# Low parts of weight blocks by a negated copy and an accumulating transfer, in a two-layer recurrent trunk

## The chip, the cores and the metric

The kernel runs on one core of a Trainium2 chip. The metric is the device time of one execution in microseconds (us); the median of several runs is compared. A core has five engines that run their own instruction streams in order and wait for each other by semaphores: TensorE (PE, matmuls), VectorE (DVE), ScalarE (ACT), GpSimd (POOL) and SyncE (SP). Transfers between the chip's memory (HBM) and the core's memory (SBUF) are issued by one of these engines into a queue and carried by 16 DMA engines.

## What is computed

The reference is one inference step of two layers on 1024 prompt tokens and 8 x 4 sample tokens (1056 columns in all), width 1024, in float32. Cut to what matters here:

```python
# layer 0, a gated linear recurrence (RG-LRU), width 1536
u = rmsnorm(x, g0) @ a_w_in            # 1024 x 3072: branch and gate
xc = causal_conv(u[:, :1536])          # 4 taps
h = scan(a(xc), b(xc))                 # gates by 96 x 96 blocks
x = x + (h * silu(u[:, 1536:])) @ a_w_out      # 1536 x 1024
# layer 1, HGRN2: linear attention with decay, 8 heads of 128
q, f, v, gate = split(rmsnorm(x, g1) @ b_w_in) # 1024 x 4096
o = chunked_recurrence(silu(q), k(f), v, decay(f))
x = x + (norm(o) * silu(gate)) @ b_w_out       # 1024 x 1024
y = rmsnorm(x, gf)
```

## The kernel before

**Three products for one.** TensorE works on float32r operands, which keep fewer bits than float32. So each operand is split in two: the high part is the value rounded to float32r, the low part is the value minus the high part. A product is made of three matmuls into one bank (mm3, lines 253 to 257): high weights by high data (L255), high weights by low data (L256), low weights by high data (L257). The weights reach the core unsplit; the split is made on the chip, block by block.

**How a weight block becomes two.** A block is a tile of 128 partitions by up to 512 columns. A load brings it into a raw tile (wraw, a ring of NRAW = 3). ScalarE copies it into a float32r tile (whi, a ring of NW = 4): that is the high part. Then GpSimd subtracts the high part from the raw tile and writes the low part (wlo, a ring of NW = 4). Two places do this with GpSimd:

- `weights` (L382 to L403), for weights used in the ordinary way, in blocks of 512, 384 or 128 columns. Its argument e names the engine of the subtraction; without a word it is GpSimd (G). For the first two weight blocks of the program e is VectorE. Where `at` is given, the parts go to named homes instead of the rings; that is so for four weights at the start and two near the end.
- `split` within `seven` (L1446 to L1454), for layer 1's projections of heads 1 to 7. `seven` computes two 1024 x 128 projections (query and gate, or value and forget gate) with seven products of half size instead of eight, after Strassen and Winograd. Each product takes one raw block of 512 columns: some as loaded, some combined of others by VectorE (`combine`, L1456 to L1458), which writes over raw tiles. There are five raw slots, the ring of three and two halves of a row of R. GpSimd's subtraction is cut there into CUT = 2 halves of 256 columns.

Three more places split weights by GpSimd with code of their own (L561, L675, L1668).

**The order of the work.** Nothing is issued as it is written. Each operation is added to a `Flow` (L52) with its engine, an estimated duration, its emitter, the keys it reads and writes, and a priority. `Flow.run` plans the whole layer as a list schedule: it simulates the five engines and one serial transfer resource (250 KB per us, plus a latency of some 2.4 to 2.6 us), computes latest start times backwards from the end, uses them as priorities, repeats this, and at last tries 3000 random changes to the order of the first 60 us. Then the operations are issued in the planned order, engine by engine. The order on an engine is fixed from there; on the chip each instruction waits only for its semaphores. An operation that is late holds up what stands behind it on its engine. A change of the estimated costs or of the list of operations changes the planned order of everything.

**Who issues what.** Layer 0's loads and most stores are issued by SP (`dma`, L324), in SP's planned order; an issue that must wait for its tile to come free holds up the issues behind it. The loads of raw blocks in `seven` are issued by ScalarE (L1441), so there they stand in ScalarE's order. GpSimd issues no transfer.

**TensorE's part in layer 1.** Each of the seven products is 24 matmuls of 264 columns in two bank fills of 12. Three banks (NM7 = 3) take turns; VectorE's additions (`plus`, L1520, L1521) and ScalarE's copies (L1493) empty them. Between the products stand the bursts of small matmuls of the recurrence, at the places that the letters b in FQ, GV0 and GV (L30) mark: a query/gate pair and a value/forget pair alternate. The digits there are the order of the seven products; a block's split is issued NW = 4 products ahead of its use.

**The recurrence between.** Of each head, the rows are scaled level by level on VectorE (`scale`, L1057), turned with the help of transfers out of the core and back (`turned`, L1175), and ScalarE collects the turned keys (L1192). GpSimd raises small rows to a power for the norms (L463, L1317) and makes the masked values (L1216).

**The end.** The output projection of layer 1 adds its product, normalises and stores; there the late weights are split by L1668.

Of the kernel before, what the change touches and what calls it, by code (L numbers as in the profile page):

```python
# [18 lines left out]
AF = mybir.ActivationFunctionType  # L19
ALU = mybir.AluOpType  # L20
# [3 lines left out]
SEARCH = 3000  # L24
NW, NXO, NRAW = 4, 3, 3
K1 = 5
NMM = 3
HC = 2
NM7 = 3
FQ, GV0, GV = "12b675b43", "126b74b35", "126b754b3"  # L30
CUT = 2
SPOTS, SPOTS0, SPOTS1 = (-1, -1, 0, 2), (2, 5, -1, -1), (1, 5, 9, 13, 17, 20)
K2 = 8 - K1
RM, SM = 3, 6
# [189 lines left out]
def tile_trunk(ctx: ExitStack, tc: tile.TileContext, xT, prm, hc, w0, wg, wo0, w1, wo1, s_in,  # L224
               yT, h_out, c_out, sp_out, ss_out):
    nc = tc.nc
    V, S, G, T, Q = nc.vector, nc.scalar, nc.gpsimd, nc.tensor, nc.sync
# [83 lines left out]
    with ExitStack() as l0:  # L311
        pl = l0.enter_context(tc.tile_pool(name="l0", bufs=1, reuse_waits="tile"))
        fl = Flow("PE")
# [10 lines left out]
        def dma(dst, src, r=(), w=(), prio=5, kb=180, q=Q):  # L324
            fl.add("SP" if q is Q else "ACT", 0.45, lambda: q.dma_start(dst, src), r, w, prio, kb * (1.0 if r or fl.exact else 0.75))

        def act(n, emit, r, w, prio=5, more=0.0):
            fl.add("ACT", (0.09 + 0.00088 * n if fl.exact else 0.25 + 0.0007 * n) + more, emit, r, w, prio)

# [7 lines left out]
        def subtract(e, n, b, x, a, r, w, prio):  # L337

            emit = lambda: e.tensor_tensor(b, x, a.bitcast(F32), op=ALU.subtract)  # L339
            if e is G:  # L340
                pool(n, emit, r, w, prio)
            else:
                dve(n, emit, r, w, prio, True)
# [38 lines left out]
        def weights(src, n, prio=2, e=G, at=None, q=Q, own=()):  # L382

            own = iter(own)
            got = []
            for a in range(0, n, 512):
                m = min(512, n - a)
                raw, *rk = next(own, None) or next(raws)
                if at:
                    (hi, hk), (lo, lk) = ((o[:, a:a + m], k) for o, k in at)  # L390
                else:
                    (hi, hk), (lo, lk) = next(his), next(los)
                dma(raw[:, :m], src[:, a:a + m], (), rk, prio, m / 2, q)
                act(m, lambda hi=hi, raw=raw, m=m: S.copy(hi[:, :m], raw[:, :m]), rk, (hk,), prio)  # L394
                subtract(e, m, lo[:, :m], raw[:, :m], hi[:, :m], (*rk, hk), (lk,), prio)
                got.append((hi, lo, hk, lk))

            def get(k):
                q = slice((k % 4) * 128, (k % 4 + 1) * 128)
                hi, lo, hk, lk = got[k // 4]  # L400
                return hi[:, q], lo[:, q], (hk, lk)

            return get  # L403
# [457 lines left out]
        raw = (halves[1][:8], [slots[i] for i in (1, 4, 7, 2, 5, 8)] + [halves[1][8], free[8]], free[:8])  # L861
# [82 lines left out]
    with ExitStack() as l1:  # L944
        p1 = l1.enter_context(tc.tile_pool(name="l1", bufs=1, reuse_waits="tile"))
        last = {e: max(t[3] for t in fl.log if t[1] == e) for e in Flow.ENGINES}
        fl = Flow(side=0.4, busy={e: max(0.0, t - last["PE"]) for e, t in last.items()})
        banks8 = [next(mm) for _ in range(4)] + [next(hg) for _ in range(4)]
        mm, hg = cycle(banks8[:NMM]), cycle(banks8[NMM:])
        ts = cycle(ks)  # L950
# [3 lines left out]
        at = fixed("attn", [128, 8, 128], F32, p1)  # L954
# [466 lines left out]
        def seven(h, a, b, order, at=()):  # L1421
# [24 lines left out]
            def split(p):  # L1446
                (raw, rk), (hi, hk), (lo, lk) = slot[named[p]], next(his), next(los)
                act(512, lambda: S.copy(hi, raw), (rk,), (hk,), 2)  # L1448
                for i in range(CUT):
                    w = slice(i * (512 // CUT), (i + 1) * (512 // CUT))  # L1450
                    subtract(G, 512 // CUT, lo[:, w], raw[:, w], hi[:, w], (rk, hk), (lk,), 2)
                parts[p] = hi, lo, (hk, lk)
                if p not in (1, 2):
                    freed.append(slot[named[p]])  # L1454
# [15 lines left out]
            for c in order:  # L1470
# [8 lines left out]
                hi, lo, wk = parts[p]  # L1479
# [36 lines left out]
                n = steps.index(p) + NW  # L1516
# [72 lines left out]
        for k in range(H):  # L1589
            if k < 4:  # L1590
                olds = [("x", 1, k, x) for x in range(2)] + [("T", 1, i, k, x) for i in range(2) for x in range(2)]
            else:
                n, i = ((2, 0), (3, 0), (4, 0), (4, 1))[k - 4]
# [18 lines left out]
        def yparts(c):  # L1612
            return [(yh[k][:, chunk(c)], yl[k][:, chunk(c)], (("yh", k, c), ("yl", k, c))) for k in range(K1)]

# [21 lines left out]
        for n, (m, c) in enumerate([(m, c) for c in range(NCH) for m in range(2)] + [(m, c) for m in range(2, KD) for c in range(NCH)]):  # L1636
            if m not in ws2:
                at_ = None
                if m < 2:
                    at_ = [(flat[m + 2, 1][:, i * 640:i * 640 + 640], ("wt", m, i)) for i in range(2)]  # L1640
                    for _, k in at_:
                        inherit(k, [("T", m + 2, 1, j, x) for j in range(4) for x in range(2)])
                ws2[m] = weights(wo1[m][:, :128 * K1], 128 * K1, at=at_)
                for k in ykeys(Y2 + m, 0, TOK):
# [15 lines left out]
        for m in range(KD):  # L1660
            row = (xh, xl)[m // 4][4 + m % 4]
            hi, lo, hk, lk = row[:, :nl], row[:, nl:2 * nl], ("late", m, 0), ("late", m, 1)
            for k in (hk, lk):
                inherit(k, [("x", p, m % 4, x) for p in (2, 3) for x in range(2)])
            raw, rk = next(raws)
            dma(raw[:, :nl], wo1[m][:, 128 * K1:], (), (rk,), 1, nl / 2)
            act(nl, lambda hi=hi, raw=raw: S.copy(hi, raw[:, :nl]), (rk,), (hk,), 1)
# [58 lines left out]
        for a, n in OUT:  # L1726
# [4 lines left out]
            for m in range(KD):  # L1731
# [5 lines left out]
                hi, lo, wk = late[m]  # L1737

                def emit(ps=ps, hi=hi, lo=lo, q=q, n=n):
                    for k in range(K2):  # L1740
                        w = slice(128 * k, 128 * k + 128)
                        mm3(ps[:, :n], (hi[:, w], lo[:, w]), yh[K1 + k][:, q], yl[K1 + k][:, q], k == 0, k == K2 - 1)

                pe(9 * n / 2200, emit, (*wk, *((o, K1 + k, c) for o in ("xh", "xl") for k in range(K2) for c in cs)), (pk,))
                x, xk = x2[m][:, q], ykeys(Y2 + m, a, n)
# [89 lines left out]
```

## Time and profile before

| what | value |
|---|---|
| time, median of 3 runs | 1047.58 us (1045.82 to 1047.79) |
| span of the profiled execution | 1045.1 us |
| its mean granted TensorE clock | 0.997 |
| HBM read, written | 85.93 MB, 38.20 MB |

The profiled execution has no time of its own besides its span; the median of the runs lies 2.5 us above that span, which is taken as what lies around it.

How to read the views. The page's first part gives each engine's busy time, its share of the span and its number of instructions; PEld is TensorE's loading of weights, beside the matmuls. The third part has the DMA queues: packets, MB, and the time of the packets as a share of 16 engines' span. The fourth follows the chain of work that ended last back from the end and says what share of the span each engine holds in it. In the groups, a row gives line, engine, operation, out<-in by the program's names, shapes, count, busy us, mean ns of one, then the idle time of the engine just before these instructions and what ended it. In the waits, a row gives who waited for whom: us in total, times, longest. In the stretches, a row gives the stretch, its length, and the busy time of PE, PEld, DVE, ACT and POOL with counts, then TensorE's granted clock, the share of the DMA engines that was busy, and GB/s; asked for one line alone, it gives that line's engine only. In the timeline, a row gives start, length, engine, line, operation, out<-in, shapes, count, and in brackets the idle time before it with its releaser; instructions that follow each other directly may be merged into one row. In the DMA issues, a row gives out<-in, the issuing queue, the count, KB each and the median us from issue to landing.

### The profile page before, as it was taken

Reading aid. Unit: us, or ns where it says so; the run is one execution under the profiler, and the core shown is the slowest. Engines: PE = TensorE matmul, PEld = TensorE weight load, DVE = VectorE, ACT = ScalarE, POOL = GpSimd, SP = SyncE. Lnnn points to the kernel's source line nnn. Section 1 sums busy time; section 2 is a strip of 40 time slices with the busy share of each in tenths; the row PEclk is TensorE's granted clock in tenths of the full one; section 3 lists DMA queues with packets and bytes.
Section 4 is the critical chain, followed back from the end, with each engine's and each line's share of the span. In section 5 each row is a group of like instructions: output and inputs, shape, how many; then the busy total and the mean of one; then the engine's idle time right before and its main releaser. Section 6 shows DMA issues by size and latency. Waiting matters only on the chain.

```text
span 1045.1 us, 25638 instructions
## 1 busy us (share of the span) xinstructions
PE 1033.6 (99%) x9860; PEld 1004.5 (96%) x9860; DVE 824.2 (79%) x1620; ACT 582.9 (56%) x1327; POOL 511.3 (49%) x587
## 2 busy tenths in 40 slices
PE   9999999999999999999999999999999999999997
PEld 9999999999999999999999999999999999999986
DVE  7999996788788689345598998988979797985436
ACT  6568656867765776334455464546463645652324
POOL 3425343544435365644517655555555565651544
PEclk9999999999999999999999999999999999999998
DMA  9201112123761586435646142423324242576204
GB/s 303 66 20 55 54 49 72 49 65 97 214 197 48 170 281 195 145 118 173 195 138 187 56 131 97 129 85 116 97 101 127 88 127 85 182 224 210 86 1 167
DMA packets 92010, 130.67 MB, mean 125 GB/s; under 512 B 11632, under 2 KB 70000, under 8 KB 91888
## 3 DMA queue, kind: packets, MB, share of 16 engines
q1 hardware_dynamic: 82096, 112.64, 34.7%
q10 hardware_dynamic: 9792, 16.40, 5.0%
q8 instruction: 77, 1.26, 0.5%
q14 instruction: 45, 0.37, 0.1%
HBM read 85.93 MB, written 38.20 MB: 119 GB/s over the span
## 4 chain that ended last, share of the span: by engine, by line
PE 88%; DVE 8%; DMA 2%; issue 1%; POOL 0%; ACTq 0%; ACT 0%; POOLq 0%; SPq 0%; DVEq 0%
PE mm L255 25%; PE mm L257 24%; PE mm L256 24%; PE hg L1075 2%; PE hg L583 1%; PE hg L1289 1%; DMA wraw<-in_w_dram 1%; PE hg L255 1%; PE hg L1291 1%; PE hg L256 1%; PE hg L257 1%; DVE a L1257 1%; DVE sg L1057 1%; DVE R L1057 1%; PE hg L1333 1%
## 5 line engine op out<-in xcount | busy, mean ns | idle before, releaser
L255 PE MATMUL mm<-xh,whi 128*128 128x352 f32 (+1 forms) x1127 | 352.5, 313 | 0.7 <-DVE k L1521 0.5
L257 PE MATMUL mm<-xh,wlo 128*128 128x352 f32 (+1 forms) x1127 | 346.9, 308 | 0.0
L256 PE MATMUL mm<-xl,whi 128*128 128x352 f32 (+1 forms) x1127 | 346.7, 308 | 0.0
L339 POOL TENSOR_TENSOR wlo<-wraw,whi 128x256 fp32r<-128x256 f32 (+3 forms) x188 | 203.9, 1100 | 207.1 <-ACT whi L394 103.0
L255 PEld LDWEIGHTS mm<-xh,whi 128*128 128x128 f32 x1127 | 211.7, 188 | 3.2 <-DVE k L1521 1.6
L256 PEld LDWEIGHTS mm<-xl,whi 128*128 128x128 f32 x1127 | 212.0, 188 | 1.5
L257 PEld LDWEIGHTS mm<-xh,wlo 128*128 128x128 f32 x1127 | 211.8, 188 | 0.0
L255 PE MATMUL mm<-t,whi 128*128 128x264 f32 (+1 forms) x330 | 96.5, 292 | 0.8 <-DVE k L1521 0.8
L515 DVE SCALAR_TENSOR_TENSOR k<-xb,prm_sb,k 128x352 f32<-128x352 f32 (+2 forms) x144 | 89.5, 633 | 9.6 <-ACT k L512 6.4
L257 PE MATMUL mm<-t,wlo 128*128 128x264 f32 (+1 forms) x330 | 94.5, 286 | 0.0
L256 PE MATMUL mm<-t,whi 128*128 128x264 f32 (+1 forms) x330 | 94.3, 286 | 0.0
L339 POOL TENSOR_TENSOR wlo<-R,whi 128x256 fp32r<-128x256 f32 x70 | 63.7, 931 | 47.6 <-ACT whi L1448 30.7
L1521 DVE TENSOR_TENSOR k<-mm,k 128x264 f32<-128x264 f32 x154 | 64.2, 423 | 16.5 <-PE mm L257 15.8
L598 POOL TENSOR_TENSOR k<-X 128x352 f32<-128x352 f32 x36 | 42.8, 1199 | 47.7 <-DVE R L599 38.8
L255 PEld LDWEIGHTS mm<-t,whi 128*128 128x128 f32 x330 | 62.0, 188 | 1.6 <-DVE k L1521 1.0
L257 PEld LDWEIGHTS mm<-t,wlo 128*128 128x128 f32 x330 | 62.1, 188 | 0.2 <-POOL wlo L339 0.2
L256 PEld LDWEIGHTS mm<-t,whi 128*128 128x128 f32 x330 | 62.1, 188 | 0.0
L394 ACT CAST whi<-wraw 128x512 fp32r<-128x512 f32 (+2 forms) x79 | 43.8, 572 | 29.9 <-PE mm L256 15.9
L1448 ACT CAST whi<-wraw 128x512 fp32r<-128x512 f32 x56 | 34.4, 616 | 33.2 <-DVE wraw L1458 13.5
L255 PE MATMUL mm<-yh,whi 128*128 128x352 f32 x153 | 49.9, 326 | 0.0
L257 PE MATMUL mm<-yh,wlo 128*128 128x352 f32 x153 | 49.4, 323 | 0.0
L256 PE MATMUL mm<-yl,whi 128*128 128x352 f32 x153 | 49.4, 323 | 0.0
(457 smaller groups left out, 2540.3 us busy)
## 6 DMA issues: line engine op xcount, KB each, us to landing
wraw<-in_w_dram SPq DMA_DIRECT2D x53, 256.0 KB, 3.1
wraw<-in_w_dram ACTq DMA_DIRECT2D x37, 256.0 KB, 2.9
wraw<-in_wo_dram SPq DMA_DIRECT2D x34, 192.0 KB, 2.5
R<-in_w_dram ACTq DMA_DIRECT2D x17, 256.0 KB, 2.9
si<-in_s_in_dram SPq DMA_DIRECT2D x8, 512.0 KB, 6.6
vt<-sg SPq DMA_DIRECT2D x8, 512.0 KB, 3.1
sg<-vt SPq DMA_DIRECT2D x32, 128.0 KB, 3.0
kt<-kt SPq DMA_DIRECT2D x8, 512.0 KB, 2.6
```

Of the source, the lines that this page charges most:

```text
L255: T.matmul(out, wh, xh, start=first, stop=False)
L256: T.matmul(out, wh, xl, start=False, stop=False)
L257: T.matmul(out, wl, xh, start=False, stop=last)
L339: emit = lambda: e.tensor_tensor(b, x, a.bitcast(F32), op=ALU.subtract)
L394: act(m, lambda hi=hi, raw=raw, m=m: S.copy(hi[:, :m], raw[:, :m]), rk, (hk,), prio)
L515: dve(u, lambda src=src, dst=dst, sh=sh, k=k: V.scalar_tensor_tensor(dst, sh(src, k), pc("cw", 12 * k + m), dst, op0=ALU.mult, op1=ALU.add ...
L583: fl.add("PE", 0.62, lambda ps=ps, i=i, c=c: T.matmul(ps[:96, :CH], gs[:, i, :], ST[:96, chunk(c)], start=True, stop=True), (("gs",), *((" ...
L598: pool(CH, lambda x=x, a=a, b=b: G.tensor_tensor(x, a.bitcast(F32), b.bitcast(F32), op=ALU.add), (ak, bk), (xk,), 3)
L1057: dve(n // 2, lambda sv=sv, dv=dv, s=s, f=f: V.tensor_tensor(dv[:, :, s, :], sv[:, :, s, :], f, op=ALU.mult), (*sk, *gk), dk if i == o els ...
L1075: T.matmul(ps[32 * j:32 * j + 32, n * w:n * w + w], B[:, o:o + 32], q(slice(o, o + 32)), start=True, stop=True, tile_position=(0, 32 * j))
L1448: act(512, lambda: S.copy(hi, raw), (rk,), (hk,), 2)
L1521: dve(QT, lambda: V.tensor_tensor(o[0], z[0], u[0], op=ALU.add), (z[1], u[1]), (o[1],), 0)
```

## The change

In `weights`, wherever the subtraction was GpSimd's and the parts go to the rings, and in `split` of `seven`, the low part is now made otherwise. ScalarE, which has just written the high part, reads the raw tile once more and writes it, scaled by -1 and rounded to float32r, into the low part's tile: the negated high part. Then GpSimd issues a transfer from the raw tile to the low part's tile with an accumulating addition, so that the tile holds raw minus high. The transfer moves the whole block at once, also in `seven`, where the subtraction was cut in two. The planner books it on GpSimd with 1.1 us and as a transfer of the block's KB. The raw tile counts as read until the transfer has landed. Blocks with homes of their own, the first blocks that VectorE makes, and the three other places are as before. FIRST = False means that layer 0 is included.

```diff
+FIRST = False
...
+        def swdge(dst, src, r, w, prio, kb, op=None):
+            more = {"accum_op": op} if op else {}
+            fl.add("POOL", 1.1, lambda: G.dma_start(dst, src, **more), r, w, prio, kb)
+
+        def remainder(n, lo, raw, r, lk, prio):
+
+            act(n, lambda: S.activation(lo, raw, AF.Copy, scale=-1.0), r, (lk,), prio)
+            swdge(lo, raw, (*r, lk), (lk,), prio, n / 2, ALU.add)
...
                 act(m, lambda hi=hi, raw=raw, m=m: S.copy(hi[:, :m], raw[:, :m]), rk, (hk,), prio)
-                subtract(e, m, lo[:, :m], raw[:, :m], hi[:, :m], (*rk, hk), (lk,), prio)
+                if e is G and at is None and not FIRST:
+                    remainder(m, lo[:, :m], raw[:, :m], rk, lk, prio)
+                else:
+                    subtract(e, m, lo[:, :m], raw[:, :m], hi[:, :m], (*rk, hk), (lk,), prio)
...
                 act(512, lambda: S.copy(hi, raw), (rk,), (hk,), 2)
-                for i in range(CUT):
-                    w = slice(i * (512 // CUT), (i + 1) * (512 // CUT))
-                    subtract(G, 512 // CUT, lo[:, w], raw[:, w], hi[:, w], (rk, hk), (lk,), 2)
+                remainder(512, lo, raw, (rk,), lk, 2)
```

## Prediction, before the change was run

> **What bounds the kernel now.** I read the page first, then TensorE's waits, then the stretches of 25 us.
>
> ```profile
> span 1045.1 us, 25638 instructions
> PE 1033.6 (99%) x9860; PEld 1004.5 (96%) x9860; DVE 824.2 (79%) x1620; ACT 582.9 (56%) x1327; POOL 511.3 (49%) x587
> q1 hardware_dynamic: 82096, 112.64, 34.7%
> PE 88%; DVE 8%; DMA 2%; issue 1%; POOL 0%; ACTq 0%; ACT 0%; POOLq 0%; SPq 0%; DVEq 0%
> ```
> ```profile
> PE mm L255 <- DVE k L1521: 2.4, 4, 1.1
> ```
> ```profile
> 900.00:925.00 25.00, 23.09 (x365) 21.93 (x364) 21.77 (x51) 12.54 (x33) 15.38 (x18) 1.00 0.62 188
> ```
> TensorE is busy in 99% of the span and holds 88% of the chain that ended last; GpSimd, whose work the change replaces, holds 0% of it. The longest entry among TensorE's waits is 2.4 us, for a VectorE addition. The one stretch with a visible hole is 900 to 925, 23.09 of 25 us, so 1.91 us idle. No wait of TensorE for a low part (wlo) is listed. So what the change can win in the steady part is about 2.4 us, whatever it frees elsewhere. What it can lose is open: a low part that comes late stops TensorE directly.
>
> **What goes.** GpSimd's subtractions of weight blocks, kept apart by shape:
>
> ```profile
> L339 POOL TENSOR_TENSOR wlo<-wraw,whi 128x256 fp32r<-128x256 f32 x112 | 102.1, 931 | 95.7 <-ACT whi L1448 73.0 <-PE mm L257 7.0 <-DVE a L1257 4.8
> L339 POOL TENSOR_TENSOR wlo<-wraw,whi 128x512 fp32r<-128x512 f32 x54 | 76.9, 1430 | 97.8 <-ACT whi L394 89.3 <-DVE X L521 3.9 <-ACT xb L507 3.1
> L339 POOL TENSOR_TENSOR wlo<-R,whi 128x256 fp32r<-128x256 f32 x70 | 63.7, 931 | 47.6 <-ACT whi L1448 30.7 <-PE mm L257 6.3 <-PE hg L1333 4.0
> L339 POOL TENSOR_TENSOR wlo<-wraw,whi 128x384 fp32r<-128x384 f32 x16 | 21.9, 1383 | 13.6 <-ACT whi L394 13.6
> L339 POOL TENSOR_TENSOR wlo<-wraw,whi 128x128 fp32r<-128x128 f32 x6 | 3.3, 547 | 0.0
> ```
> Two halves of 256 make one block, so there are (112 + 70) / 2 = 91 blocks in layer 1's seven-product stage and 54 + 16 + 6 = 76 elsewhere: 167. They took 102.1 + 76.9 + 63.7 + 21.9 + 3.3 = 267.9 us of GpSimd, of which nothing was on the path. What this can free is VectorE, in this stretch of its timeline:
>
> ```profile
> 907.12 0.71 DVE L1057 TENSOR_TENSOR R<-R,sg 128x528 f32<-128x528 f32 x1
> 908.21 2.90 DVE L1057 TENSOR_TENSOR sg<-a,sg 128x528 f32<-128x528 f32 x1
> ```
> The same operation took 0.71 and 2.90 us, and it did so in the stretch with the hole. I book -1.0 us for it, between 0 (the hole may have another cause) and -2.4. The Trainium skill (SBUF — State Buffer, Who interferes with whom) says that a VectorE instruction with two SBUF inputs and a GpSimd instruction that reads SBUF block each other fully; these two rows agree with it, and descriptor writing, which reads no SBUF operand, would not block this way.
>
> **What comes on ScalarE.** One more pass per block, the same size as the high part's cast:
>
> ```profile
> L394 ACT CAST whi<-wraw 128x512 fp32r<-128x512 f32 x57 | 34.7, 618 | 29.6 <-PE mm L256 15.9 <-DMA wraw<-in_w_dram 7.8 <-issue 1.8
> L1448 ACT CAST whi<-wraw 128x512 fp32r<-128x512 f32 x56 | 34.4, 616 | 33.2 <-DVE wraw L1458 13.5 <-PE mm L256 12.7 <-PE mm L257 4.4
> L1448 ACT CAST whi<-R 128x512 fp32r<-128x512 f32 x35 | 21.7, 621 | 28.5 <-PE mm L256 17.2 <-POOL wlo L339 6.0 <-PE mm L257 4.4
> L394 ACT CAST whi<-wraw 128x384 fp32r<-128x384 f32 x16 | 7.8, 512 | 0.1
> ```
> That is (91 + 54) x 0.62 + 16 x 0.51 = 98 us, and some 2 us for the six small blocks: ScalarE goes from 583 to about 683 us, 65% of the span. The low part's buffer is freed by L257, the matmul just behind the L256 that already frees the high part's, so the second pass adds its own length and hardly a wait. Behind it on ScalarE stand the copies that empty PSUM banks and the next loads' issues. Tightest is the recurrence of layer 0, by the stretches for all engines and for L394 alone:
>
> ```profile
> 350.00:375.00 25.00, 25.00 (x149) 23.79 (x148) 19.67 (x33) 22.84 (x37) 12.94 (x11) 1.00 0.73 225
> ```
> ```profile
> 275.00:300.00 25.00, 3.90 (x7) 1.00 0.85 261
> 300.00:325.00 25.00, 2.46 (x4) 1.00 0.30 87
> 350.00:375.00 25.00, 2.34 (x5) 1.00 0.73 225
> 375.00:400.00 25.00, 2.49 (x4) 1.00 0.89 287
> 400.00:425.00 25.00, 0.00 (x0) 1.00 0.58 167
> ```
> From 350 to 375 ScalarE has 22.84 of 25 us, and the five casts there come again: 22.84 + 2.34 = 25.18. It is full for one stretch, by 0.2 us, which the next stretches can take. Zero.
>
> **What comes on the transfers.** No transfer issued by GpSimd and no accumulating one is in this trace. The nearest are these, the last from the stretch 668 to 690 alone:
>
> ```profile
> wraw<-in_w_dram ACTq DMA_DIRECT2D x37, 256.0 KB, 2.9
> yd<-sg SPq DMA_DIRECT2D x6, 528.0 KB, 7.7
> kt<-kt SPq DMA_DIRECT2D x8, 512.0 KB, 2.6
> ```
> ```profile
> wraw<-in_w_dram ACTq DMA_DIRECT2D x3, 256.0 KB, 5.7
> ```
> Queue q1 moved 112.64 MB in 34.7% of 1045.1 us, 0.31 MB/us, so one pass over a block of 256 KB (0.262 MB) costs 0.84 us of all engines. An accumulation has to read what it adds to: I take one pass more than the load's 2.9, so 3.7 us to landing, between 2.6 and 7.7. In layer 0, seven blocks from 275 to 300 (I take 0.22 MB each) with two passes are 7 x 0.22 x 2 / 0.31 = 9.9 us of transfer beside a share of 0.85: 1.24, 6 us too many; from 375 to 400 four full blocks are 4 x 2 x 0.84 = 6.7, a share of 0.89 + 0.27 = 1.16, 4 us too many. The stretches behind them have shares of 0.30 and 0.58, so the excess can flow off while the loaded tiles last. I take +1.0, between 0 and +10.
>
> **The time from cast to low part, layer 1.** Issue on GpSimd: between the 0.33 us of a ScalarE issue and the 2 x 0.93 of the halves it replaces; I take 1.1, the middle, which the diff's planner books too. Cast, second pass, issue, landing: 0.62 + 0.62 + 1.1 + 3.7 = 6.0 us, between 0.62 + 0.62 + 0.33 + 2.6 = 4.2 and 0.62 + 0.62 + 1.86 + 7.7 = 10.8. The room is from a block's cast to its first matmul:
>
> ```profile
> 561.41 1.13 ACT L1448 CAST whi<-wraw 128x512 fp32r<-128x512 f32 x2
> 680.88 0.61 ACT L1448 CAST whi<-wraw 128x512 fp32r<-128x512 f32 x1
> 681.63 2.40 POOL L339 TENSOR_TENSOR wlo<-wraw,whi 128x256 fp32r<-128x256 f32 x2 [3.27 <-PE mm L1095]
> 684.06 0.33 ACTq L325 DMA_DIRECT2D wraw<-in_w_dram  x1
> 684.44 0.62 ACT L1448 CAST whi<-R 128x512 fp32r<-128x512 f32 x1 [2.94 <-POOL wlo L339]
> 846.89 0.61 ACT L1448 CAST whi<-wraw 128x512 fp32r<-128x512 f32 x1
> ```
> ```profile
> 566.72 0.28 PE L255 MATMUL mm<-t,whi 128*128 128x264 f32 x1
> 687.55 0.28 PE L255 MATMUL mm<-t,whi 128*128 128x264 f32 x1
> 854.05 0.28 PE L255 MATMUL mm<-t,whi 128*128 128x264 f32 x1
> ```
> Casts and products stand in the same order, so the k-th of the 91 pairs up. The shortest room is 566.72 - 561.41 = 5.31 us; then come four blocks of one kind (product 4 of a value/gate pair, one each in four heads), the first with 687.55 - 680.88 = 6.67, the last with 854.05 - 846.89 = 7.16. Today the low part was ready 684.03 - 680.88 = 3.15 us after its cast. With 6.0 us one block is late, by 0.7. But these four run beside the key and state transfers, where the load took 5.7 instead of 2.9: 6.0 + 2.8 = 8.8 there makes them late by 2.1 to 1.6, 7.5 in all. So 0.7 to 8.2; I take +4.0.
>
> **Waits that are lengthened.** A raw block is free only at landing, no longer at the subtraction's end.
>
> ```profile
> SPq L325 <- POOL wlo L339: 85.8, 43, 8.3
> ```
> In layer 0 SP's queue already waits 43 times for a low part before it reloads a raw block; behind it wait the loads and stores of the residual. In layer 1 the reload stands in ScalarE's own order: above, ScalarE sat 2.94 us until the subtraction ended at 684.03, issued the load and went on at 684.44. The new landing would be 680.88 + 6.0 = 686.9, so 2.8 us later if the issue stays at that place. The planner reorders by its own costs, so I book this inside the 4.0. VectorE's combinations (L1458) overwrite raw blocks and wait for the landing too; queued behind them are the additions (L1521) that free the three product banks.
>
> **The sum.** -1.0 + 1.0 + 4.0 = +4.0 on the span of 1045.1: 1049.1. The median of the runs is 1047.58, 2.5 above that span, so the forecast is 1051.6; I write 1051.5.
>
> **Rivals.** *All hidden.* If landing takes 2.6 us as the kt row has it, a block needs 0.62 + 0.62 + 1.1 + 2.6 = 4.9 us, under the shortest room of 5.31: nothing is late, and with layer 0's excess absorbed the time stays within 1 of 1047. Against it: the kt row moves data once and adds nothing. The Trainium skill (DMA: Bandwidth & Descriptors, Anatomy of one DMA) gives about 2.0 us plus bytes over 436 GB/s for a GpSimd-issued transfer, which for 256 KB makes an estimate of 2.6 us; by that page this rival would win. No run here shows such a transfer yet. *Faster.* Low parts in time as above, and VectorE, no longer held up as at 908.21, closes its 2.4 us of waits: 1047.6 - 2.4 = 1045.2. It decides where the 2.90 us row falls back to 0.71, and only if a block needs under 5.3 us. *Transfers collide.* Both excesses of layer 0 reach TensorE (+10), and the four late blocks with the first cost their 8.2: 1047.6 + 18 = 1066. For it: shares of 0.85 and 0.89; against it: the empty stretches behind. *GpSimd not relieved.* If an issue holds it for the 1.6 us that a block took (267.9 / 167), its busy time stays at 511; L would be 6.5 and the time that of the forecast.
>
> **Chances.** Forecast 0.40 (1049.7 to 1056), hidden 0.20, faster 0.20, collision 0.20 (1056 to 1075). This kernel's measurement tells about 0.2%, 2.1 us, from no change, so: slower 0.60 (0.40 + 0.20), same 0.20, faster 0.20. The range leaves out the collision's upper part and the last of the faster cases: 1044.5 to 1065. Slower alone would be 1049.7 to 1065.
>
> **What would show it.** Right: a new queue with about 41 MB read ((145 x 256 + 16 x 192 + 6 x 64) KB), GpSimd's L339 groups on wlo gone, ScalarE near 683, and new TensorE waits for a DMA on wlo from 560 on, largest in the four blocks named. Wrong: landings under 3 us with no such wait (hidden); TensorE's hole at 900 closed and the rest unchanged (faster); holes in layer 0 near 290 and 390 of several us (collision). A changed order of the opening or the last 20 us, which the planner's search may give, is in no term and would upset the sum by as much as it moves them.

## The result, and the profile after

The changed kernel takes 1064.47 us (median of 4 runs, 1060.5 to 1068.22) against 1046.87 (4 runs of the kernel before beside it): ratio 1.0166, interval 1.0145 to 1.0186, slower by 17.6 us. The profiled execution took 1061.77 us, with a span of 1060.0. The four executions fall into two pairs, 1060.5 and 1061.77 us at a mean granted clock (TensorE's, as a share of full speed) of 0.996 and 1067.16 and 1068.22 us at 0.993 and 0.994, so the median lies between the pairs, and the profiled execution, from which the stages below are read, is one of the faster pair.

First the page of the changed kernel: span, engines, two DMA queues, the landing of the new transfers.

```profile
span 1060.0 us, 25806 instructions
PE 1040.3 (98%) x9860; PEld 1009.7 (95%) x9860; DVE 753.1 (71%) x1620; ACT 661.8 (62%) x1494; POOL 402.4 (38%) x496
q1 hardware_dynamic: 82096, 112.64, 34.0%
q0 software_dynamic: 24048, 41.56, 23.3%
wlo<-wraw POOLq DMA_DIRECT2D x110, 256.0 KB, 4.3
wlo<-R POOLq DMA_DIRECT2D x35, 256.0 KB, 4.3
```

GpSimd fell from 511.3 to 402.4 us and VectorE from 824.2 to 753.1; ScalarE rose from 582.9 to 661.8. A new queue, q0, moved 41.56 MB and holds the 16 engines for 23.3% of the span. TensorE's busy time has grown by 6.7 us, the span by 14.9.

TensorE's waits, in the same kernel (us in total, times, longest):

```profile
PE mm L258 <- DMA wlo<-wraw: 3.7, 3, 2.0
PE mm L258 <- DMA wlo<-R: 3.6, 3, 1.9
PE mm L256 <- DVE sg L556: 2.4, 1, 2.4
```

The low part is a wait now, 7.3 us in six places. Where they stand, from its timeline:

```profile
34.73 0.43 PE L256 MATMUL mm<-xh,yh 128*128 128x352 f32 x1 [2.36 <-DVE sg L556]
...
403.44 0.43 PE L258 MATMUL mm<-xh,wlo 128*128 128x352 f32 x1 [1.28 <-DMA wlo<-wraw]
...
577.58 0.39 PE L258 MATMUL mm<-t,wlo 128*128 128x264 f32 x1 [1.95 <-DMA wlo<-wraw]
645.53 0.39 PE L258 MATMUL mm<-t,wlo 128*128 128x264 f32 x1 [1.89 <-DMA wlo<-R]
701.43 0.39 PE L258 MATMUL mm<-t,wlo 128*128 128x264 f32 x1 [0.45 <-DMA wlo<-wraw]
757.39 0.39 PE L258 MATMUL mm<-t,wlo 128*128 128x264 f32 x1 [0.59 <-DMA wlo<-R]
813.82 0.39 PE L258 MATMUL mm<-t,wlo 128*128 128x264 f32 x1 [1.10 <-DMA wlo<-R]
```

One in layer 0, one in the first value/gate pair of layer 1, and one, always in product 4, in the value/gate pair of heads 2 to 5: 1.3 us and 6.0 us. The 2.36 us at 34.73 is no low part: there TensorE waits for VectorE in the opening.

Three stretches of the changed kernel beside those shown of before (same columns):

```profile
275.00:300.00 25.00, 25.00 (x152) 24.14 (x151) 20.73 (x30) 22.07 (x36) 9.47 (x11) 1.00 0.95 269
375.00:400.00 25.00, 25.00 (x155) 24.74 (x154) 18.71 (x33) 19.28 (x34) 7.99 (x8) 1.00 0.99 280
914.11:939.11 25.00, 24.50 (x376) 23.49 (x375) 20.21 (x53) 15.11 (x38) 12.15 (x16) 1.00 0.94 248
```

The shares of 0.85 and 0.89 became 0.95 and 0.99: the transfer engines are busy nearly all the time there. The last stretch stands for 900 to 925 of before, which ended 4.49 us behind the start of the last matmul of 264 columns; that matmul starts 14.11 us later now (its rows follow), so the same work is found from 914.11 to 939.11. Of the hole of 1.91 us it has 0.50 left.

To see which stage the time went to, two points serve that every kernel here has: the start of its first product of 264 columns (the seven-product stage of layer 1 begins) and the start of the last such matmul. Before:

```profile
560.85 0.28 PE L255 MATMUL mm<-xh,whi 128*128 128x264 f32 x1
...
920.51 0.28 PE L257 MATMUL mm<-xh,wlo 128*128 128x264 f32 x1
```

After:

```profile
569.34 0.29 PE L256 MATMUL mm<-xh,whi 128*128 128x264 f32 x1
...
934.62 0.29 PE L258 MATMUL mm<-xh,wlo 128*128 128x264 f32 x1
```

So 8.5 us are lost ahead of the stage, 5.6 inside it (365.28 against 359.66), 0.8 behind it: 14.9. The experiments' table is made of the same two rows of each trace; "ahead", "stage" and "behind" are differences to the kernel before, in us, and their sum is the difference of the spans.

| kernel | median us | ratio (interval) | ahead | stage | behind |
|---|---|---|---|---|---|
| changed | 1064.47 | 1.0166 (1.0145–1.0186) | +8.5 | +5.6 | +0.8 |
| old_order_new_work | 1194.2 | 1.1414 (1.1391–1.1437) | +42.5 | +100.6 | +4.0 |
| new_order_old_work | 1057.02 | 1.0090 (1.0077–1.0103) | +7.2 | +0.7 | +1.2 |
| new_order_subtract | 1059.52 | 1.0116 (1.0102–1.0129) | +8.0 | +3.5 | +1.8 |
| new_order_pass_only | 1050.66 | 1.0033 (1.0021–1.0044) | +5.7 | −3.0 | +0.6 |
| new_order_plain_copy | 1053.24 | 1.0066 (1.0053–1.0079) | +8.3 | +0.3 | +0.4 |
| layer0_only | 1057.46 | 1.0101 (1.0087–1.0116) | +7.6 | +0.1 | +1.2 |
| layer1_only | 1055.86 | 1.0079 (1.0062–1.0097) | −0.2 | +9.8 | −0.9 |
| planner_two_passes | 1082.78 | 1.0327 (1.0313–1.0341) | +17.9 | +11.3 | +6.7 |
| planner_later_landing | 1058.59 | 1.0108 (1.0091–1.0124) | +10.2 | +3.9 | −0.3 |
| layer1_later_landing | 1049.24 | 1.0021 (1.0011–1.0032) | −0.1 | +2.9 | −0.8 |
| layer1_three_of_seven | 1046.24 | 0.9988 (0.9980–0.9997) | +1.6 | −0.8 | −0.7 |
| before_other_seed | 1052.96 | 1.0052 (1.0040–1.0064) | +5.5 | 0.0 | +1.0 |
| before_seed_3 | 1052.19 | 1.0050 (1.0035–1.0065) | +5.0 | +0.1 | +0.8 |
| before_seed_4 | 1055.62 | 1.0080 (1.0061–1.0099) | +7.2 | +2.4 | −0.2 |
| changed_seed_2 | 1066.89 | 1.0184 (1.0151–1.0217) | +11.3 | +8.7 | +0.7 |
| changed_seed_3 | 1065.74 | 1.0163 (1.0136–1.0190) | +9.1 | +11.9 | +0.8 |

A stage time is of one execution; layer1_three_of_seven and layer1_later_landing have the order of before ahead of the stage and show +1.6 and −0.1, so a reading ahead of it is good to some 1.5 us. In the profiled executions of new_order_old_work, new_order_subtract, new_order_plain_copy and before_seed_4 the granted clock is 0.93 between 25 and 50 us, where before and changed have 1.00: that is 25 x 0.07 = 1.7 us of their "ahead".

### The profile page after: what moved, and what is told of

Read it like the earlier page. It is cut to its first block, busy times and chain, and to the rows that moved or that the text cites. A ratio compares the mean times of both kernels' runs of the same rounds, so it can differ in the third digit from the quotient of the medians.

```text
span 1060.0 us, 25806 instructions
## 1 busy us (share of the span) xinstructions
PE 1040.3 (98%) x9860; PEld 1009.7 (95%) x9860; DVE 753.1 (71%) x1620; ACT 661.8 (62%) x1494; POOL 402.4 (38%) x496
## 3 DMA queue, kind: packets, MB, share of 16 engines
q0 software_dynamic: 24048, 41.56, 23.3%
## 5 line engine op out<-in xcount | busy, mean ns | idle before, releaser
L330 POOL DMA_DIRECT2D wlo<-wraw x132 | 118.0, 928 | 289.1 <-ACT wlo L334 223.7
L334 ACT ACTIVATE wlo<-wraw 128x512 fp32r<-128x512 f32 (+2 forms) x132 | 77.9, 600 | 72.3 <-PE mm L258 42.8
L528 DVE SCALAR_TENSOR_TENSOR k<-xb,prm_sb,k 128x352 f32<-128x352 f32 (+2 forms) x144 | 79.8, 559 | 19.9 <-ACT k L525 13.2
L1532 DVE TENSOR_TENSOR k<-mm,k 128x264 f32<-128x264 f32 x154 | 63.9, 425 | 16.6 <-PE mm L258 15.1
L611 POOL TENSOR_TENSOR k<-X 128x352 f32<-128x352 f32 x36 | 45.0, 1281 | 42.8 <-DVE R L612 30.2
L330 POOL DMA_DIRECT2D wlo<-R x35 | 30.6, 875 | 65.4 <-ACT wlo L334 52.5
```

The costliest lines, as they stand in the source:

```text
L330: fl.add("POOL", 1.1, lambda: G.dma_start(dst, src, **more), r, w, prio, kb)
L334: act(n, lambda: S.activation(lo, raw, AF.Copy, scale=-1.0), r, (lk,), prio)
L528: dve(u, lambda src=src, dst=dst, sh=sh, k=k: V.scalar_tensor_tensor(dst, sh(src, k), pc("cw", 12 * k + m), dst, op0=ALU.mult, op1=ALU.add ...
L611: pool(CH, lambda x=x, a=a, b=b: G.tensor_tensor(x, a.bitcast(F32), b.bitcast(F32), op=ALU.add), (ak, bk), (xk,), 3)
L1532: dve(QT, lambda: V.tensor_tensor(o[0], z[0], u[0], op=ALU.add), (z[1], u[1]), (o[1],), 0)
```

## The experiments

The change does two things at once: it gives the engines other work, and it gives the planner other costs, so that the planner writes another order for every engine. The theory at the start was that the work costs the time (late transfers); its rival was the order. The first runs part the two.

### Old order with new work, new order with old work

Every engine keeps the order of before; where GpSimd's subtraction stood, the new pass and transfer are put (cut short; in the seven products, where the subtraction had two halves, the pass stands at the place of the first half and the transfer at that of the second):

```diff
-    pool(n, lambda: G.tensor_tensor(lo, raw, hi, op=ALU.subtract), ...)
+    pool(n, lambda: (S.activation(lo, raw, AF.Copy, scale=-1.0),
+                     G.dma_start(lo, raw, accum_op=ALU.add)), ...)
```

> Every engine keeps the order of the kernel before, instruction for instruction; only the work is new: where GpSimd's subtraction of a block stood, ScalarE gets the negated pass and GpSimd issues the accumulating transfer. Theory 'late transfers': the order left about 3.15 us from a cast to its low part and now gets 6 to 9, so it loses at least what the changed kernel loses behind its opening, 1047 + 15 = 1062, up to 1075, since nothing was moved earlier to meet it. Rival 'order': 1047 to 1050, since the work itself would cost next to nothing.

Measured: 1194.2 us, +146, far over what was expected. ScalarE's waits and TensorE's in this run:

```profile
ACT k L1509 <- DMA wlo<-wraw: 27.5, 8, 5.2
...
ACT whi L1466 <- DMA wlo<-R: 23.0, 5, 6.0
```
```profile
PE mm L255 <- DVE k L1537: 43.1, 14, 7.1
PE mm L255 <- ACT k L1509: 18.8, 8, 3.8
PE mm L257 <- DMA wlo<-wraw: 15.3, 6, 7.0
```

ScalarE has no use for a low part. It waits for one because the next load into the raw block stands in its order, and the copies behind that load wait with it. TensorE then waits mostly for VectorE and ScalarE, to free its banks, and only third for the low part itself. The seven-product stage (which loses 100.6 us), of before and then of this run:

```profile
560.85:920.51 359.66, 358.17 (x5137) 344.83 (x5135) 311.35 (x645) 189.50 (x502) 206.96 (x247) 1.00 0.36 113
```
```profile
603.39:1063.69 460.30, 390.40 (x5137) 372.57 (x5135) 280.03 (x657) 234.20 (x596) 124.86 (x160) 0.92 0.58 141
```

TensorE is idle there for 69.9 us instead of 1.5. The other 32.2 us of the loss are busy time: the same 5137 matmuls took 390.40 us instead of 358.17, at a granted clock of 0.92 instead of 1.00. So the work is dear in this order, and the planner's new order hides nearly all of it. The other half (cut short):

```diff
-    act(n, lambda: S.activation(lo, raw, AF.Copy, scale=-1.0), r, (lk,), prio)
-    swdge(lo, raw, (*r, lk), (lk,), prio, n / 2, ALU.add)
+    act(n, lambda: None, r, (lk,), prio)
+    fl.add("POOL", 1.1, lambda: G.tensor_tensor(lo, raw, hi, op=ALU.subtract), ...)
```

> Every engine keeps the order that the planner gave the changed kernel, instruction for instruction, but the low parts are made as before the change: the negated pass is issued as nothing, and in the place of the transfer GpSimd subtracts the whole block of 512 columns (1.43 us). Theory 'late transfers' (the loss of 17.6 us is made by what the new work does on the chip: landings of 4.3 us and more, transfer shares of 0.95 and over, the second ScalarE pass): only the opening's 2.6 us, which stands in the order, is left: 1047 + 2.6 = 1049.5, between 1047.5 and 1052, and no TensorE wait for a low part. Rival 'order' (the planner's new order of all engines is worse by itself): 1060 to 1064.

Measured: 1057.02. This is not yet the old work: in the new order many negated passes stand ahead of their block's cast, and there the subtraction read the buffer's older high part and the cast waited for it. The next run puts the cast at whichever of the two places comes first:

> A mend of the run in the new order: the trace of the changed kernel lets many blocks run their negated pass ahead of their cast, so that there the subtraction stood ahead of the cast in the order, read the buffer's older content and held the cast up. Now the first of a block's two places on ScalarE makes the cast, the second nothing, and GpSimd subtracts 512 columns at the place of the transfer: the changed kernel's order on all engines with the old work. Theory 'order in part' (the planned order costs the opening and some of layer 0, the transfers cost layer 1): 1050 to 1055, all of it lost ahead of the first product of 264 columns, nothing behind it. Rival 'late transfers only': 1047 to 1050. Rival 'order alone': 1060 to 1064.

Measured: 1059.52, above the range of "order in part" and just under that of "order alone". Ahead of the stage it loses 8.0 us (1.7 of them by the lower clock between 25 and 50 us) of the 8.5 that the changed kernel loses there, without any transfer. What it loses in the stage (3.5) has no wait for a low part, but TensorE waits five times for VectorE's additions (L1539, 2.6 us in all). That this order keeps no place for a subtraction of 1.4 us where 1.1 was booked is argued, not shown.

### The new order with the transfer taken out, then put back in part

```diff
-    fl.add("POOL", 1.1, lambda: G.dma_start(dst, src, **more), r, w, prio, kb)
+    fl.add("POOL", 1.1, lambda: None, r, w, prio, kb)
```

> The changed kernel without its transfers: the same order, the negated pass on ScalarE writes the low part, and GpSimd issues nothing (the addition of the raw block is left out). Against the run before it this adds 98 us of ScalarE and takes 268 us of GpSimd away. Theory 'order in part': the pass costs nothing of its own, so the same time as the run before it within 2 us; all that the changed kernel loses beyond it (to 1064.5) is the transfers'. Rival 'ScalarE': the second pass, waiting for the low part's buffer in ScalarE's order (37 waits, 61.8 us, longest 5.7 in the changed kernel), holds up the PSUM copies: 1058 to 1064.

Measured: 1050.66. Same order, same passes of ScalarE, no transfers: 13.8 us of the 17.6 are gone by the medians, 11.6 of the 14.9 by the spans. "Order in part" missed too: it expected the time of the run before this one, 1059.5 within 2 us, so that in this order the subtractions themselves cost 8.9. The stage is 3.0 us shorter than in the kernel before. "ScalarE" falls as a cause, although the passes do wait; from the changed kernel's waits of ScalarE:

```profile
ACT wlo L334 <- PE mm L258: 61.8, 37, 5.7
```

In the run without transfers these waits are 61.0 us in 49 places, and they cost nothing that can be seen. And 5.7 us are lost ahead of the stage with no transfer at all. Only 1.7 of them are idle time of TensorE (3.5 us against 1.8), and from 100 to 500 us it is never idle. One stretch, of before and then of this run:

```profile
200.00:250.00 50.00, 50.00 (x313) 49.76 (x313) 44.42 (x65) 35.48 (x69) 24.95 (x28) 1.00 0.21 60
```
```profile
200.00:250.00 50.00, 50.00 (x309) 49.51 (x308) 38.57 (x59) 41.18 (x81) 12.22 (x16) 1.00 0.19 55
```

Both are busy for all 50 us, but one gets 313 matmuls done and the other 309, at the same granted clock. The pace goes with the order: layer1_only, which has the order of before there, gets 314 done in this stretch, and before_other_seed, the work of before in another order, 309. So between two orders a busy share alone doesn't show the pace; what slows the matmuls was not found. Next the transfer alone, copying instead of adding:

```diff
-    swdge(lo, raw, (*r, lk), (lk,), prio, n / 2, ALU.add)
+    swdge(lo, raw, (*r, lk), (lk,), prio, n / 2)
```

> The changed kernel, with the transfer copying instead of accumulating (what is left out is the addition; order and all else are the same). Theory 'landing': a landing of one pass is 1 to 1.5 us shorter than the accumulating one's median of 4.3 us, the queue's share falls from 23.3% to about 13 to 16%, and of layer 1's 6 us some 3 to 5 go: 1059 to 1062. Rival 'accumulation is free': 1064.5, landing 4.3, share 23%.

Measured: 1053.24, lower than the range expected. Its queue and landings on the page, and its issues on GpSimd by line (ns, min/median/max):

```profile
q0 software_dynamic: 24048, 41.56, 13.4%
wlo<-wraw POOLq DMA_DIRECT2D x110, 256.0 KB, 3.0
wlo<-R POOLq DMA_DIRECT2D x35, 256.0 KB, 4.1
```
```profile
L330 POOL DMA_DIRECT2D wlo<-wraw x132: 527/540/761, 87.5 to 986.8; - x132
```

And the same line of the changed kernel:

```profile
L330 POOL DMA_DIRECT2D wlo<-wraw x132: 850/882/1589, 84.9 to 992.2; - x132
```

The same 41.56 MB hold the engines for 0.134 x 1054.1 = 141 us when copied and 0.233 x 1060.0 = 247 us when added, 1.75 times as long; an issue takes 0.88 us instead of 0.54, a landing 4.3 instead of 3.0 (110 blocks) and 4.1 (the 35 from R). The longest landing is no shorter: 9.4 us when copied, 9.1 when added. By the medians, moving the blocks costs 1053.24 − 1050.66 = 2.6 us and adding 1064.47 − 1053.24 = 11.2. By the spans it is 5.7 and 5.9; but the profiled execution of the plain copy lost some 2.5 us more than the two others in its first 50 us, where its granted clock was lower, and without these it is 3.2 and 8.4. Either way adding costs more than moving.

### Each layer alone

Layer 1's 91 blocks alone: `FIRST = True`, so that the other blocks are subtracted.

> Only the 91 blocks of layer 1's seven-product stage have the new low part; the other 76 blocks go back to GpSimd's subtraction. From the comparison of the two traces at equal TensorE work (8.5 us lost by the first product of that stage, 6 us behind it): theory 'late transfers' gives the 6 us of layer 1 alone: 1047 + 6 = 1053, between 1050 and 1056. Rival 'ScalarE and transfers of layer 0 are the main cost, layer 1's late blocks follow from a start that was late already': 1047 to 1049.

Measured: 1055.86, +8.1, all of it in the stage. The rival falls: layer 1 loses its time from a start that is not late. Of TensorE's waits in this run 4.0 us are for low parts and 3.4 for VectorE's additions (L1532). The complement puts the subtraction in halves back into the seven products:

> The complement of the run with layer 1 alone: the 76 blocks ahead of and behind the seven-product stage have the new low part, the 91 of that stage are subtracted by GpSimd as before. Theory 'parts add': what the changed kernel had lost by the first product of 264 columns (2.6 us in the opening, some 3 by the order, 3 by the transfers, 8.5 in all) and nothing behind it: 1047.3 + 8.5 = 1056, between 1053 and 1058. With the 8.2 us of layer 1 alone that adds up to the 17.2 of both. Rival 'one feeds the other' (a late start makes layer 1's blocks late): 1048 to 1052.

Measured: 1057.46, +10.2 and none in the stage. The two add up to 18.3, about the 17.6 of both together: no sign that one feeds the other. Its one wait for a transfer is the place that the changed kernel has at 403:

```profile
402.99 0.43 PE L258 MATMUL mm<-xh,wlo 128*128 128x352 f32 x1 [2.00 <-DMA wlo<-wraw]
```

### What the planner books

Accumulating transfers booked with twice their bytes (`n` in place of `n / 2`):

> The changed kernel, with one number changed in the planner's book: an accumulating transfer is booked with twice its bytes, so that a block of 256 KB has a lag of 2.15 + 512/250 = 4.2 us from the end of its issue, the landing that the trace showed as the median (4.3), instead of 3.2. Theory 'late transfers': the planner puts casts earlier, the late blocks of layer 1 go or shrink, 1064.5 - 6 = 1058.5 (between 1054 and 1062). Rival 'full resources' (transfer engines and ScalarE are filled up, so no order helps): 1063 to 1068.

Measured: 1082.78, 18 us worse than the changed kernel: a miss for both. The account of bytes also decides when the planner believes other transfers to land, so this edit moved more than the lag. Booking the lag alone:

```diff
-        return (self.HOPS[a[0]] ...
+        late = 1.1 if a[0] == "POOL" and a[5] else 0.0
+        return late + (self.HOPS[a[0]] ...
```

(The two long lines are cut short.)

> The changed kernel, with one number in the planner's book: from the end of a GpSimd issue to whoever uses the landed block it books 1.1 us more (4.3 instead of 3.2), and leaves its account of the transfers' bytes as it is. With twice the bytes booked the planner's order came out 18 us longer than the changed kernel. Theory 'lag': only the lag was booked wrongly, and this repairs layer 1's late blocks: 1056 to 1060. Rival 'full resources': any later use of the low parts only moves the wait to the buffers (raw, high and low rings of 3 and 4 blocks), 1063 to 1085.

Measured: 1058.59, −5.9; the stage went from +5.6 to +3.9 in the profiled executions. The same with layer 1 alone, whose layer 0 is that of before:

> Only layer 1's 91 blocks have the new low part, and the planner books 1.1 us more from the end of a GpSimd issue to the use of the landed block. Layer 0 as before the change. Theory 'lag' (layer 1's loss is a landing booked too short): the 8.2 us shrink to 2 to 5: 1049 to 1052. Rival 'no order helps': 1055 to 1057.

Measured: 1049.24: from +8.1 to +2.0. "Lag" holds: most of layer 1's loss was a landing booked too early. The waits for low parts that are left, 3.3 us in four places, stand in value/gate pairs again. The changed kernel's worst block, beside the key and state transfers, was issued at 636.34; its landing, from the answer for that moment alone:

```profile
si<-in_s_in_dram SPq DMA_DIRECT2D x1, 512.0 KB, 9.6
wlo<-R POOLq DMA_DIRECT2D x1, 256.0 KB, 9.1
```

9.1 us, beside a load of 512 KB that took 9.6: TensorE's wait at 645.53 ends there. So those blocks were left to GpSimd's subtraction:

```diff
-                remainder(512, lo, raw, (rk,), lk, 2)
+                if p in (1, 2, 7):
+                    remainder(512, lo, raw, (rk,), lk, 2)
+                for i in range(0 if p in (1, 2, 7) else CUT):
...
+                    subtract(G, 512 // CUT, lo[:, w], raw[:, w], hi[:, w], (rk, hk), (lk,), 2)
```

> Only in layer 1's seven-product stage, and there only products 1, 2 and 7 of each seven have the new low part (39 blocks); products 3 to 6, whose landings were 5 to 9 us beside the key and state transfers, are subtracted by GpSimd in halves as before; the planner books 1.1 us more behind a GpSimd issue. Theory 'only the late blocks cost': nothing is late, and VectorE is relieved in part, as in the run without transfers, which won 2.7 us in this stage: 1045 to 1048. Rival 'transfers lengthen the loads and holds of buffers whichever blocks they serve': 1049 to 1053.

Measured: 1046.24, ratio 0.9988, interval 0.9980 to 0.9997. Its median is 0.12% under that of the kernel before, less than the 0.2% taken as a difference that can be told, so the loss is gone and a gain is not shown. None of its TensorE waits is for a low part, and the landings in the stage are short:

```profile
wlo<-wraw POOLq DMA_DIRECT2D x29, 256.0 KB, 3.6
wlo<-R POOLq DMA_DIRECT2D x8, 256.0 KB, 3.6
```

### Is the order's loss the change's?

The order of the opening and layer 0 comes out of a random search in the planner. Another seed, nothing else:

```diff
-        rng = Random(1)
+        rng = Random(2)
```

> The kernel before, with another seed in the random search of the planner, so another order in the opening and nothing else. Theory 'order is a lottery': the 2.6 us that the changed kernel loses in the opening are within what any new search gives, so this run moves by 1 us or more: 1045 to 1050, not 1047. Rival 'the opening's loss belongs to the change': 1046.5 to 1048.

Measured: 1052.96, +5.7, above both ranges, with the same number of instructions on every engine (9860, 1620, 1327 and 587 on TensorE, VectorE, ScalarE and GpSimd) in another order. Its two points:

```profile
566.30 0.28 PE L255 MATMUL mm<-xh,whi 128*128 128x264 f32 x1
...
925.92 0.28 PE L257 MATMUL mm<-xh,wlo 128*128 128x264 f32 x1
```

+5.5 ahead of the stage and 0.0 in it: the run without transfers lost 5.7 in the same place. Two more seeds of this kernel, and two of the changed one (a draw is the order that one seed gives):

> The kernel before with a third seed in the planner's random search. Theory 'luck of the search': the order of the kernel before is a good draw, and another draw loses several us in the opening and layer 0, as the second seed did (5.7): 1049 to 1054. Rival 'the second seed was the bad draw': 1046 to 1048.

> The same with a fourth seed. Theory 'luck of the search': 1048 to 1054. Rival 'the second seed was the bad draw': 1046 to 1048.

> The changed kernel with a second seed in the planner's search. Theory 'luck of the search': the 5.6 us that its order loses ahead of layer 1 are a draw and not part of the change, so other seeds move it by several us: 1058 to 1066, and the difference in layer 1 stays. Rival 'the change forces this order' (with the new costs any order is longer in the opening and layer 0): 1062 to 1066.

> The same with a third seed. Theory 'luck of the search': 1058 to 1066, apart from the second seed's by 2 us or more. Rival 'the change forces this order': 1062 to 1066.

Measured: 1052.19 and 1055.62 (in and above the ranges of "luck of the search"); 1066.89 and 1065.74. Seed 1 gave the kernel before the best of four draws, by 5.3 to 8.8 us. The changed kernel's three draws lie within 2.5 us, with intervals that overlap. "Apart by 2 us or more" was a miss (1.2), and 1066.89 lies above both ranges, so whether the change by itself forces a slower order was not told apart: ahead of the stage the changed kernel's draws lose 8.5, 11.3 and 9.1 us, the other three of before 5.5, 5.0 and 7.2. The mean of these three of before is 1053.6, that of the changed kernel's three 1065.7: the change itself costs about 12 us, and the other 5.5 of the 17.6 are the lost draw. With seed 1 counted in, the mean of before is 1051.9, and it is about 14 and 4. The order held still gives about the same: changed kernel minus the run without transfers is 2.8 ahead of the stage, 8.6 in it, 0.2 behind, 11.6 by the spans, where both have a granted clock of 1.00 up to the stage's end, and 13.8 by the medians.

A late low part can cost more than the wait. In changed_seed_3 the block that is 1.89 us late in the changed kernel at 645.53 is 3.20 us late, and this is the stretch behind it:

```profile
647.40:650.80 3.40, 3.40 (x15) 3.40 (x16) 0.68 (x3) 1.08 (x4) 0.00 (x0) 0.50 0.51 128
```

The granted clock is 0.50 for 3.4 us, which is another 1.7 us; behind the 1.89 us of the changed kernel it stays at 1.00. Not every wait of more than 2 us is followed by this: the 2.36 us at 34.73 are not in the changed kernel, and in the plain copy the same wait is.

## Why the prediction failed

The sign was right and most of the places, the size was not: +4.0 forecast, +14.9 in the span. Of the 10.9 us between them 7.5 lie ahead of the stage (8.5 against the +1.0 booked there), 2.6 in it (5.6 against −1.0 + 4.0) and 0.8 behind it. By its own steps:

**The terms of the sum.** Forecast −1.0 + 1.0 + 4.0.

*VectorE's relief*, −1.0 (0 to −2.4): the row it was booked from was misread. What GpSimd did beside the 2.90 us at 908.21 of before is this:

```profile
907.17 1.70 POOL L1216 TENSOR_TENSOR vb<-vst,bm 96x256 fp32r<-96x256 f32 x2 [1.31 <-DVE vst L1203]
908.83 1.71 POOL L339 TENSOR_TENSOR t<-wraw,t 128x128 fp32r<-128x128 f32 x2
```

Those are masked values and a weight with a home of its own (t), and the change leaves both on GpSimd. Nor does the hole need the change's work to close: in new_order_subtract, where GpSimd still subtracts, the same work (911.48 to 936.48) has 0.19 us idle. So the new order closes it with the subtractions still there. A relief is shown elsewhere: with the order held still, the stage is 6.4 us shorter without the subtractions (new_order_pass_only against new_order_subtract), and the waits for VectorE's additions are gone. Against the kernel before it is 3.0 us shorter, of which the order's part is not known. As far as a gain came, the row that it was booked from did not show it: that is luck.

- *Layer 0's transfers*, +1.0 (0 to +10): 569.34 − 566.50 = +2.8 against the run without transfers, 1.3 of it the wait at 403.44. The two places named by their shares became 0.95 and 0.99. The excess flowed off as far as can be seen, with about 3 us lost.
- *Layer 1's late low parts*, +4.0 (0.7 to 8.2): this is one of the two steps that failed. The mechanism was right, and nearly the places: the first pair and product 4 of a value/gate pair in four heads (heads 2 to 5; the rows had named 3 to 6), 6.0 us of waits. The price was too small: with the order held still, the transfers cost the stage 8.6 us, over the upper end, and layer 1 alone loses 9.8 in its stage. The median block needed no more than was booked (landing 4.3 us from the start of an issue, against 1.1 + 3.7 = 4.8). What was mis-sized is the block beside the key and state transfers: the load's +2.8 us was taken for it, and it landed after up to 9.1 us instead of 4.8 + 2.8 = 7.6. Of the 8.6 us 2.6 are in no wait for a low part: 0.5 is idle time ahead of L1088, and 2.1 are longer busy time (358.79 us against 356.68), whose cause stays open.

**The term that was left out**, the new order, is the other step that failed, and the larger one. The prediction said that a changed order "is in no term and would upset the sum by as much as it moves them"; it moved them by 5.7 us. The sum had been made as if the order of before stayed, apart from the passes put in. With that order kept, the run shows +146 us instead of +4.0; with another order, each of three draws of the unchanged kernel loses 5.0 to 7.2 us ahead of the stage (1.7 of the 7.2 by the lower clock). Neither is near the sum that was booked. Why these orders are slower is known only in part: 1.7 of the 5.7 us are idle time, the rest is a slower pace of the matmuls, whose cause stays open.

**The second pass**, "its own length and hardly a wait": it waited 61.8 us in 37 places, so the wait was misjudged, and the cost of nothing still came out right: with the passes and no transfer the loss ahead of the stage (5.7) is that of the other draws of before (5.0 to 7.2), which have no passes. ScalarE reached 661.8 us, 21 under the forecast.

**Reloads in ScalarE's order**, "2.8 us later if the issue stays at that place": shown by the old order, where ScalarE waits up to 6.0 us for a low part that it doesn't use. That the planner would move them was right too.

**The rivals.** *All hidden* needed a landing of 2.6 us. That figure is also an estimate from the Trainium skill (DMA: Bandwidth & Descriptors, Anatomy of one DMA), whose fit for a transfer issued by GpSimd, 2.0 us plus bytes over 436 GB/s, gives 2.6 us for 256 KB. The plain copy came near it with medians of 3.0 and 4.1 us, the accumulating one with 4.3 did not. By the medians 11.2 us of time lie between the two runs. *Faster* rested on the misread rows at 908. *GpSimd not relieved* is refuted, 511.3 to 402.4 us, with 0.88 us for an issue against 1.1 booked. *Collision* came near the total with 1066, from the wrong parts: layer 0's transfers cost 2.8, not 10.

Two passes over a block were the right guess for what accumulation takes of the transfer engines: 247 us / 41.56 MB x 0.262 MB = 1.56 us a block, against 2 x 0.84 = 1.68.

## What to carry to other kernels

Where a search writes the order, price the change and the new draw apart: run the unchanged kernel with two or three other seeds first, since a good draw (here 5 to 9 us) can be lost by any edit that touches a cost. An accumulating transfer moved work off an engine here at the price of nearly two passes and a landing that doubled beside large transfers (4.3 to 9.1 us); give it only to blocks whose use is far off, and book the measured landing. And when a buffer is freed by a transfer instead of an engine, look for the loads into it that stand in another engine's order, because that engine will wait for a result it has no use for. Before a slow row is booked as what a change frees, look at what the other engine did beside it.

## What was not expected of the hardware

The addition in a transfer slows its issue as well: 0.88 us on GpSimd against 0.54 for the same blocks copied, and 1.75 times the time on the transfer engines. In the place shown, 1.03 us went by from the start of a negated pass to the start of the issue that waited for it, of which the pass is 0.63:

```profile
637.40 0.63 ACT L334 ACTIVATE wlo<-wraw 128x512 fp32r<-128x512 f32 x1
```
```profile
638.43 0.86 POOL L330 DMA_DIRECT2D wlo<-wraw  x1 [1.21 <-ACT wlo L334]
```
